# First left operands split straight from PSUM, softmax heads after the stick-breaking heads, and grouped first panels

## The chip, the cores and the metric

The kernel runs on one core of a Trainium2 chip. The metric is the device time of one execution in microseconds (us), as the median of several runs.

## The reference, cut to what matters

A two-layer decoder trunk on one sequence of 2048 tokens and 1024 channels, in float32. Layer 0 ("even") has four softmax heads with a forgetting bias and four stick-breaking heads, 128 wide; layer 1 ("odd") has three groups of eight dilated window heads, 64 wide.

```python
def even_layer(x, g_norm, w_in, b_f, g_q, g_k, w_out):
    proj = rmsnorm(x, g_norm) @ w_in                    # 1024 x 4100
    fq, fk, fv, f_logit, sq, sk, sv, gate = jnp.split(proj, ...)
    fox = forgetting_attention(rmsnorm(fq, g_q), rmsnorm(fk, g_k), fv, log_sigmoid(f_logit + b_f))
    sb = stick_breaking_attention(sq, sk, sv)           # w = beta * prod of (1 - beta) of later keys
    return x + (concat(fox, sb) * silu(gate)) @ w_out   # 1024 x 1024
def odd_layer(x, g_norm, w_in, g_q, g_k, w_out):
    q, k, v, gate = jnp.split(rmsnorm(x, g_norm) @ w_in, ...)   # 1024 x 5120
    att = dilated_window_attention(rmsnorm(q, g_q), rmsnorm(k, g_k), v)
    return x + (att * silu(gate)) @ w_out
```

## The kernel before, in words

**Number form.** Every operand of a large matmul is kept as two parts, hi (a rounded copy, made by ScalarE or GpSimd) and lo (the rest, made by VectorE or GpSimd by a subtraction); `K.split` makes both. A product then is three matmuls (`K.mm3`, L91 to L93: hi·hi, hi·lo, lo·hi).

**Panels.** A projection is done in two rounds of 1024 tokens (`ROUND`), and in each round in panels of 512 output columns. A panel is one 2x2 block multiplication in seven products (Strassen-Winograd): the left operands `A[A11] A[A12] A[S2] A[S3] A[S1] A[A22] A[S4]` are blocks of 512x512 of the activations or sums of them, and each has a weight operand made the same way from the panel's four weight blocks `b11 b12 b21 b22`. `panel` (L240 on) runs the seven products in the order A11, S2, A12, S3, S1, A22, S4 and adds the parts up: `u` and `u3` are kept sums, `result` gives one finished quarter to `emit`, which writes it to DRAM. A product has 24 matmuls 512 wide (mode "d": sq, sk, g0, g1) or 48 matmuls 256 wide (mode "t").

**Weights.** `Weights` loads the four blocks of a panel into four buffers `wraw` (512 KB each), makes sums in place on GpSimd (L210) and splits them into `wop` tiles, two for each product, of which there are four buffers; so weights are at most two products ahead of the matmuls.

**Left operands.** `left_direct` makes the seven left operands of the first round of layer 0 from x: the eight token tiles (`xa`: 0 to 3, `xb`: 4 to 7) are normalised by VectorE, transposed by TensorE (L137), multiplied by the gain when they are copied out of PSUM into `fa` and `fb`, and then split. A11 and A12 need only `xa`; the other five need both. `left` makes the operands of all other rounds from a transposed copy in DRAM (`hT`, or `mixT` for the mixed heads): `stage` holds the first block, `lp` tiles the pieces of the second. In the odd layer's second round it works without a stage.

**The sequence.** `even_projection` (two rounds of the panels sq, sk, sv, fv, fk, fq, g0, g1), then `even_attention` (32 softmax units, kind "f", then 32 stick-breaking units, kind "s"; each unit is 256 queries of one head), then `odd_layer`: two rounds of the output projection (two panels each, `residual` adds x and stores x1), with `transpose_to` normalising and transposing x1 into `hT` for the odd projection, two rounds of the odd projection (ten panels each) with the dilated attention between the products, and the final merge. In a unit `qk` makes the scores and weights (`rows`), and `pv`, two units later, transposes them (L785), splits them (`pT`) and multiplies them with the values into `po`. In the softmax units VectorE adds the bias and takes the running maximum (L740); in the stick-breaking units ScalarE makes two sigmoids (L746, L747) and VectorE a scan (L750).

**Order.** Instructions of one engine run in the order in which they stand. The order comes from a list scheduler of the framework, which follows the program order as priority, with `high_priority` for the evictions of PSUM (`plus`, `copy`). PSUM has four banks "s" (products, scores, `po`) and four banks "t" (transposes and others). DMAs are all issued by one queue (SP), in its order.

Of the kernel before, what the change touches and what calls it, by code (L numbers as in the profile page):

```python
# [17 lines left out]
P = 128  # L18
# [18 lines left out]
class K:  # L37
# [57 lines left out]
    def rstd(self, ss, n, width):  # L95

        nc, sm = self.nc, self.small
# [71 lines left out]

A11, A12, S2, S3, S1, A22, S4 = range(7)  # L170
ORDER = (A11, S2, A12, S3, S1, A22, S4)
FIRST = (A11, A12, S2, S3, S1, A22, S4)
ROUND = S // 2
# [3 lines left out]
class Weights:  # L177


    def __init__(self, k, panels, first=False):  # L180
        self.k, self.ready, self.first = k, [], first
        self.loads = ((w, seg, i, q) for i, (w, seg) in enumerate(panels) for q in ("11", "12", "22", "21"))
        self.raw = {}
        self.loaded = 0
        self.gen = self.prepare(panels)

    def load(self, upto):
        nc = self.k.nc
        while self.loaded < upto:
            self.loaded += 1  # L190
            nxt = next(self.loads, None)
            if nxt is None:
                return
            w, seg, i, q = nxt
            n = sum(c[1] for c in seg[0])
            raw = self.k.raws.tile([P, 4, n], F32, name="wraw", tag="raw")
            rows = slice(0, CH) if q[0] == "1" else slice(CH, D)
            at = 0
            for c0, m in seg[int(q[1]) - 1]:
                nc.sync.dma_start(raw[:, :, at:at + m], w[rows, c0:c0 + m].rearrange("(k p) n -> p k n", p=P))  # L200
                at += m
            self.raw[i, q] = raw

    def prepare(self, panels):
        k, nc = self.k, self.k.nc
        for i, (w, seg) in enumerate(panels):
            n = sum(c[1] for c in seg[0])
            self.load(4 * i + 4)
            b11, b21, b12, b22 = [self.raw.pop((i, q)) for q in ("11", "21", "12", "22")]
# [8 lines left out]
            for j, (src, work) in enumerate(steps[a] for a in (FIRST if self.first and i == 0 else ORDER)):  # L218
                for h in range(2):
                    s = slice(2 * h, 2 * h + 2)  # L220
                    for args in work:
                        tt(*args, s)
                    t = k.wps.tile([P, 2, 2, n], F32R, name="wop", tag="wp")
                    k.split(t[:, :, 0], t[:, :, 1], src[:, s], "act", "pool" if j in (1, 3, 5) else "dve")
                    self.ready.append(t)
                    yield
                if j >= 3:
                    self.load(4 * i + 2 + j)
# [9 lines left out]

def panel(k, A, W, mode, emit, tick, after=None, n=256, first=False):

# [51 lines left out]
    def kept(name):  # L292
        t = k.w4([P, ng, width], name=name, tag=name)
        return [t[:, g] for g in range(ng)]

    u, u3 = kept("u"), kept("u3")
# [99 lines left out]
def left_direct(k, x, A):  # L396

    nc = k.nc
    tt = lambda o, a, b, op: nc.vector.tensor_tensor(o, a, b, op=op)

    def load(xs, b):
        for t in range(TPC):
            for z in range(2):
                c = slice(z * CH, (z + 1) * CH)
                nc.sync.dma_start(xs[:, t, c], x[(b * TPC + t) * P:(b * TPC + t + 1) * P, c])

    def transposed(xt, F, i, on_dve=()):
        k.transposed(xt, k.ge, lambda z: F[:, z * 4:(z + 1) * 4, i], on_dve=on_dve)

    def put(j, i, src, hi_on="pool"):  # L410
        k.split(A[j][:, :, 0, i], A[j][:, :, 1, i], src, hi_on, "dve")

    xa, xb = (k.big([P, TPC, D], name=n) for n in ("xa", "xb"))
    load(xa, 0)
    yield
    load(xb, 1)
    fb, fa = (k.big([P, KT, CH], name=n) for n in ("fb", "fa"))
    A.extend([None] * 7)
    new = lambda *js: [A.__setitem__(j, k.big([P, 4, 2, CH], F32R, name=f"A{j}")) for j in js]
    new(A11, A12, S2)  # L420
    tiles = [xa[:, t] for t in range(TPC)] + [xb[:, t] for t in range(TPC)]
    k.normalise(tiles[0], "dve")
    for t, xt in enumerate(tiles):
        i = slice(t % TPC * P, (t % TPC + 1) * P)
        if t + 1 < len(tiles):
            k.normalise(tiles[t + 1], "dve")
# [5 lines left out]
        transposed(xt, fb, i)  # L432
        s = k.c2([P, 4, P], name="s2")
        tt(s, fb[:, :4, i], fb[:, 4:, i], OP.add)
        tt(s, s, fa[:, :4, i], OP.subtract)
        put(S2, i, s, "act")
    for j, src in ((S3, fa[:, :4]), (S1, fb[:, :4]), (A22, fb[:, 4:]), (S4, fa[:, 4:])):
        new(j)
        for kk in range(4):
            if j == S3:  # L440
                tt(fa[:, kk], fa[:, kk], fb[:, kk], OP.subtract)
            if j == S1:
                nc.gpsimd.tensor_tensor(fb[:, kk], fb[:, kk], fb[:, 4 + kk], op=OP.add)
            if j == A22:
                nc.gpsimd.tensor_tensor(fa[:, 4 + kk], fa[:, 4 + kk], fb[:, 4 + kk], op=OP.subtract)
            if j == S4:
                nc.gpsimd.tensor_tensor(fa[:, 4 + kk], fa[:, 4 + kk], fa[:, kk], op=OP.add)
            k.split(A[j][:, kk, 0], A[j][:, kk, 1], src[:, kk], "act", "dve")


def constants(k, cp, even_norm, odd_norm, even_b_f, even_q_gain, even_k_gain, odd_q_gain, odd_k_gain):
# [4 lines left out]
    k.ident = cs.tile([P, P], F32, name="ident")  # L456
    nc.vector.tensor_scalar(k.ident, jp, 0.0, None, op0=OP.is_equal)
# [87 lines left out]
def even_projection(k, x, w, first, first_left):  # L545
# [14 lines left out]
    def spare():  # L560
        turn[0] += 1
        return ring[0][:, turn[0] % KT]
# [3 lines left out]
    def qk_fox(dst, gain):  # L566
# [5 lines left out]
        def one(block, half, g, src, rs):  # L572
# [8 lines left out]
            k.split(hl[0], hl[1], pt, scale=gain)  # L581
# [39 lines left out]
    def forget():  # L621
# [28 lines left out]
        ("fk", plain(512), "t", qk_fox(k.fT["k"], k.gk)),  # L650
        ("fq", plain(0), "t", qk_fox(k.fT["q"], k.gq)),
# [3 lines left out]
    W = Weights(k, [(w, seg) for _ in range(2) for _, seg, _, _ in kinds], True)  # L655
    W.ahead(1)
    for _ in first:
        pass
    A = first_left
    tick = Pace()  # L660
    tick.every = 2
    for r in range(2):
        B = []
        nxt = left(k, T, 1, B)
        ring[0] = k.big([P, KT, CH], F32R, name="ring")
        for name, seg, mode, emit in kinds:
            if r == 0 and name == "fv":
                tick.add(staggered(k.transpose_to(T, x, t, k.ge) for t in range(TPC * 2, NTT)))
            last = r == 0 and name == "g1"
            panel(k, A, W, mode, emit, tick, (lambda j: next(nxt)) if last else None,  # L670
                  258 if name == "fv" else 256, r == 0 and name == "sq")
# [17 lines left out]
def even_attention(k, tail):  # L689
# [81 lines left out]
    def pv(kind, h, u, rows):  # L771

        vt = heads[kind, h][1]
        po = k.ps("s")
# [31 lines left out]
    k.table()  # L806
# [11 lines left out]
    units = [(kind, h, u) for kind in "fs" for h in range(4) for u in range(NU)]  # L818
    order = [(kind, h) for kind in "fs" for h in range(4)]
# [6 lines left out]
    for n, (kind, h, u) in enumerate(units):  # L826
# [3 lines left out]
        if n + 1 < len(units):  # L830
            q = load_q(*units[n + 1])
        nxt = order.index((kind, h)) + 1
# [12 lines left out]
    tail()  # L845
# [4 lines left out]
def odd_layer(k, x, x1, even_w_out, w_in, w_out, out):  # L850
# [7 lines left out]
    W = Weights(k, outs * 2 + [(w_in, cols(*j)) for js in rounds for j in js])  # L858
    A = []
    yield W, (left(k, k.mixT, 0, A))  # L860
# [13 lines left out]

    for r in range(2):
# [358 lines left out]
```

## Time and profile before

| | |
|---|---|
| median of 3 runs | 2847.14 us (2842.7 to 2855.95) |
| the profiled execution | 2848.43 us, its span 2846.3 us |
| mean granted TensorE clock | 0.98 |
| TensorE busy | 2678.1 us (94%) |
| VectorE busy | 2051.4 us (72%) |
| ScalarE busy | 1649.6 us (58%) |
| GpSimd busy | 1247.2 us (44%) |
| DMA | 437.37 MB, mean 154 GB/s |

Busy times are from the profile's first part. TensorE is PE there, its weight load PEld, VectorE DVE, ScalarE ACT, GpSimd POOL, the DMA queue SPq. A stall of TensorE is seen in three ways: as idle time in a table of stretches, as a row of the waits (who waited for whom, in total, how often, the longest), and as fewer matmuls in a stretch than TensorE does at its full rate.

### The profile page before, as it was taken

The page shows a single profiled execution, that of the slowest core. Times are in us where ns is not written, and L with a number is a line of the kernel's source. Part 1 is how long each engine was busy: PE and PEld are TensorE (multiplying, and loading weights), DVE is VectorE, ACT ScalarE, POOL GpSimd, SP SyncE. Part 2 cuts the span into 40 slices and gives each one's busy share as a digit, 9 for nine tenths or more (in the row PEclk, how much of TensorE's full clock was granted, in tenths as well). Part 3 has the DMA queues.
Part 4 walks back from the last instruction along what each step waited for, and adds up shares of the span by engine and source line. Part 5 has one row for each costly group of instructions (what it writes and reads, how often), then busy time and mean ns, then how long its engine had stood idle before and what let it go on. Part 6 is the DMA issues. An engine that isn't in the chain of part 4 may idle for free.

```text
span 2846.3 us, 55611 instructions
## 1 busy us (share of the span) xinstructions
PE 2678.1 (94%) x20191; PEld 2452.8 (86%) x20191; DVE 2051.4 (72%) x4384; ACT 1649.6 (58%) x3992; POOL 1247.2 (44%) x996
## 2 busy tenths in 40 slices
PE   4999999999999999998887999999989999999998
PEld 3899878998799988887887999999989999999877
DVE  7747885566588788888957857566697586763876
ACT  5446454465466677776364565555665577665642
POOL 5545465444233254456645645353345442422322
PEclk9999999999999999998998999999999999999999
DMA  3557535535644444313667463434533445444675
GB/s 119 167 165 239 189 126 178 163 120 177 189 138 138 138 130 123 112 60 93 200 218 224 144 186 114 131 102 148 173 113 107 142 143 169 127 146 139 214 248 194
DMA packets 388161, 437.37 MB, mean 154 GB/s; under 512 B 31472, under 2 KB 319536, under 8 KB 387888
## 3 DMA queue, kind: packets, MB, share of 16 engines
q1 hardware_dynamic: 387888, 433.83, 48.0%
q8 instruction: 159, 2.61, 0.4%
q14 instruction: 114, 0.93, 0.1%
HBM read 279.16 MB, written 154.57 MB: 152 GB/s over the span
## 4 chain that ended last, share of the span: by engine, by line
PE 46%; DVE 16%; DMA 6%; ACT 4%; issue 3%; POOL 1%; SPq 0%; DVEq 0%; ACTq 0%; POOLq 0%
PE ps L91 12%; PE ps L92 12%; PE ps L93 12%; PE ps L785 3%; DVE rest L750 2%; PE ps L1038 2%; PE ps L1028 2%; DVE wop L86 2%; PE ps L1009 1%; DVE S L86 1%; PE ps L954 1%; DVE A L86 1%; DVE pT L86 1%; DVE lp L319 1%; DMA fin<-uu 1%
## 5 line engine op out<-in xcount | busy, mean ns | idle before, releaser
L210 POOL TENSOR_TENSOR wraw<-wraw 128x512 f32<-128x512 f32 (+1 forms) x320 | 445.3, 1399 | 482.8 <-DVE wop L86 194.2
L81 ACT ACTIVATE wop<-wraw 128x512 fp32r<-128x512 f32 (+1 forms) x560 | 350.6, 630 | 368.0 <-PE ps L93 304.4
L86 POOL TENSOR_TENSOR wop<-wraw,wop 128x512 fp32r<-128x512 f32 (+1 forms) x240 | 329.4, 1375 | 505.6 <-ACT wop L81 484.8
L91 PE MATMUL ps<-wop,S 128*128 128x256 f32 (+1 forms) x1792 | 518.9, 290 | 18.3 <-DVE c L277 9.6
L92 PE MATMUL ps<-wop,S 128*128 128x256 f32 (+1 forms) x1792 | 513.6, 287 | 10.8 <-DVE wop L86 8.1
L92 PE MATMUL ps<-wop,A 128*128 128x256 f32 (+1 forms) x1792 | 512.2, 286 | 8.0 <-DVE wop L86 5.8
L91 PE MATMUL ps<-wop,A 128*128 128x256 f32 (+1 forms) x1792 | 511.3, 286 | 6.4 <-ACT u L282 3.1
L93 PE MATMUL ps<-wop,S 128*128 128x256 f32 (+1 forms) x1792 | 513.9, 287 | 0.0
L93 PE MATMUL ps<-wop,A 128*128 128x256 f32 (+1 forms) x1792 | 509.2, 284 | 0.0
L86 DVE TENSOR_TENSOR wop<-wraw,wop 128x512 fp32r<-128x512 f32 (+1 forms) x320 | 268.9, 841 | 236.1 <-ACT wop L81 233.4
L91 PEld LDWEIGHTS ps<-wop,S 128*128 128x128 f32 x1792 | 343.1, 192 | 24.0 <-DVE c L277 9.9
L92 PEld LDWEIGHTS ps<-wop,S 128*128 128x128 f32 x1792 | 344.5, 192 | 13.7 <-DVE wop L86 9.0
L92 PEld LDWEIGHTS ps<-wop,A 128*128 128x128 f32 x1792 | 342.9, 191 | 10.0 <-DVE wop L86 6.7
L91 PEld LDWEIGHTS ps<-wop,A 128*128 128x128 f32 x1792 | 341.2, 191 | 11.1 <-issue 4.0
L93 PEld LDWEIGHTS ps<-wop,S 128*128 128x128 f32 x1792 | 344.2, 192 | 3.3 <-issue 2.6
L93 PEld LDWEIGHTS ps<-wop,A 128*128 128x128 f32 x1792 | 343.0, 191 | 1.4 <-issue 0.9
L277 DVE TENSOR_TENSOR c<-u,ps 128x512 f32<-128x512 f32 (+1 forms) x254 | 165.1, 657 | 95.6 <-PE ps L93 86.7
L81 ACT ACTIVATE pT<-ps 128x512 fp32r<-128x512 f32 (+2 forms) x352 | 162.4, 504 | 119.0 <-PE ps L785 65.5
L753 POOL TENSOR_TENSOR rows<-rows,rest 128x512 f32<-128x512 f32 (+4 forms) x160 | 153.3, 966 | 153.1 <-DVE rest L750 147.3
L1021 ACT ACTIVATE row<-row,nm 128x256 f32<-128x256 f32 (+1 forms) x384 | 172.4, 451 | 59.1 <-DVE nm L1019 58.6
L86 DVE TENSOR_TENSOR pT<-ps,pT 128x512 fp32r<-128x512 f32 (+2 forms) x352 | 186.5, 559 | 24.6 <-ACT pT L81 23.5
L92 PE MATMUL ps<-pT,vt 128*128 128x256 f32 (+1 forms) x576 | 177.1, 308 | 7.6 <-DVE pT L86 7.3
(216 smaller groups left out, 6557.6 us busy)
## 6 DMA issues: line engine op xcount, KB each, us to landing
wraw<-in_odd_w_in_dram SPq DMA_DIRECT2D x80, 512.0 KB, 4.1
wraw<-in_even_w_in_dram SPq DMA_DIRECT2D x64, 512.0 KB, 4.5
ld<-qk SPq DMA_DIRECT2D x106, 256.0 KB, 3.3
qk<-c SPq DMA_DIRECT2D x96, 256.0 KB, 2.4
lp<-hT SPq DMA_DIRECT2D x60, 256.0 KB, 3.5
uu<-ot SPq DMA_DIRECT2D x96, 132.0 KB, 1.9
fin<-uu SPq DMA_DIRECT2D x16, 792.0 KB, 4.6
hT<-te SPq DMA_DIRECT2D x48, 256.0 KB, 4.2
```

Of the source, the lines that this page charges most:

```text
L81: nc.scalar.activation(hi, src, AF.Copy)
L86: (nc.vector if lo_on == "dve" else nc.gpsimd).tensor_tensor(lo, src, hi.bitcast(F32), op=OP.subtract)
L91: mm(out, a[0], b[0], start=start, stop=False, skip_group_check=more)
L92: mm(out, a[0], b[1], start=False, stop=False, skip_group_check=more)
L93: mm(out, a[1], b[0], start=False, stop=stop, skip_group_check=more)
L210: tt = lambda e, o, x, y, op, s: e.tensor_tensor(o[:, s], x[:, s], y[:, s], op=op)
L277: nc.vector.tensor_tensor(out[g], x[g], y[g], op=OP.add)
L750: nc.vector.tensor_tensor_scan(o[:, b:b + n][:, ::-1], back, k.ident[:, :1].to_broadcast([P, n]), 1.0 if carry is None else carry, OP.mult ...
L753: nc.gpsimd.tensor_tensor(dst[:, :w], dst[:, :w], o[:, b + 1:b + 1 + w], op=OP.mult)
L785: nc.tensor.transpose(pt[:, (jx * 2 + i) * P:(jx * 2 + i + 1) * P], rows[:, i, (jj * 2 + jx) * P:(jj * 2 + jx + 1) * P], k.ident)
L1021: nc.scalar.activation(row[:, h // 2, h % 2, :nk], row[:, h // 2, h % 2, :nk], AF.Exp, bias=nm[:, h:h + 1], accum_out=ot[:, HW + HG + h:HW ...
L1028: nc.tensor.transpose(pp[:, i * P:(i + 1) * P], row[:, h // 2, h % 2, b], k.ident)
```

## The change

1. **First left operands from PSUM.** The gain is loaded as a row to all partitions (`gb`) and multiplied into the tile together with the root on VectorE, so that the transposed tile in PSUM is final: the hi part (ScalarE) and the lo part (VectorE) are made from PSUM. The squares of two tiles share one chain for their roots. x comes in whole tiles, the weights follow right behind `xa`, and the small constants come after the first panels' first products (`late`, `identity`).
2. **Groups.** `Weights` takes group sizes. In a group, the products A11 and A12 of all its panels come first, and the five others of each panel follow; the blocks b11 and b21 are loaded a second time for them (22 more loads of 512 KB). Groups are the first three panels of layer 0, the two panels of each output round, and the first two panels of each odd round. In a group's panel A12 goes to banks of its own and is added to `u` by VectorE, where before the products were summed in PSUM and copied out by ScalarE.
3. **Left operands beside the group.** The second half of `left_direct` and the later pieces of the first `left` of the odd layer are stepped by `Pace` between these first products. `tail`, which makes the first operands of the output projection, is called in units 5 and 6 of the last head instead of after the last unit.
4. **Heads.** The stick-breaking heads come first, the softmax heads last; `po` of the stick-breaking units takes a "t" bank. The activation tables are loaded by hand at other places (9 loads stand in the program, 23 before).

```diff
-    k.normalise(tiles[0], "dve")
-    for t, xt in enumerate(tiles):
...
-            transposed(xt, fa, i, (1,))
-            put(A11, i, fa[:, :4, i])
-            put(A12, i, fa[:, 4:, i])
+    squares(0)
+    ahead = {0: (1,), 1: (2, 3), 3: (4, 5), 5: (6, 7)}
+    for t in range(2 * TPC):
+        scaled(t)
+        if t in ahead:
+            squares(*ahead[t])
+        p0, p1 = transposed(t)
         if t < TPC:
+            for z, j in enumerate((A11, A12)):
+                put(j, i, (p0, p1)[z])
+                nc.scalar.activation(fa[:, z * 4:(z + 1) * 4, i], (p0, p1)[z], AF.Copy)
+            if t == TPC - 1:
+                yield
             continue
+        nc.scalar.activation(s1, p0, AF.Copy)
+        tt(a, a, p0, sub)
+        tt(s, p1, a, sub)
+        put(S2, i, s)
+        put(A22, i, p1)
+        tt(s1, p1, s1, plus)
+        tt(fa[:, 4:, i], fa[:, 4:, i], s, sub, nc.gpsimd)
+        yield
...
 class Weights:
+            if n == 1:
+                self.parts.append((these[0], ORDER))
+            else:
+                self.parts += [(i, EARLY) for i in these] + [(i, FIRST[2:]) for i in these]
...
     if first:
         result(0, 0, u, product(A12, fresh()))
+        yield
+        u3 = kept("u3")
         plus(u, u, product(S2, fresh()))
...
-    W = Weights(k, [(w, seg) for _ in range(2) for _, seg, _, _ in kinds], True)
+    W = Weights(k, [(w, seg) for _ in range(2) for _, seg, _, _ in kinds], [3] + [1] * 13)
+    opened = [panel_steps(k, A, W, mode, emit, pace, first=tag) for (_, _, mode, emit), tag in zip(kinds, tags)]
+    for p in opened:
+        next(p)
+    late()
+    pace.finish()
...
-        po = k.ps("s")
+        po = k.ps("s" if kind == "f" else "t")
...
-    units = [(kind, h, u) for kind in "fs" for h in range(4) for u in range(NU)]
+    units = [(kind, h, u) for kind in "sf" for h in range(4) for u in range(NU)]
...
-    tail()
+        if nxt == len(order) and u in (5, 6):
+            tail()
...
-        for n in range(2):
-            panel(k, A, W, "t", residual(r, n), tick, (lambda j: next(nxt)) if n == 1 else None)
-            if r == 1 and n == 0:
-                tick.finish()
+        both = two(A, [residual(r, n) for n in range(2)], pace if r == 0 else tick,
+                   lambda j: None if j in EARLY else next(nxt))
+        next(both)
+        if r == 0:
+            pace.finish()
+            next(nxt)
+            next(nxt)
+        next(both)
+        if r == 1:
+            tick.finish()
+            next(nxt)
+            next(nxt)
+        next(both)
```

TensorE at the program's start, before: `ident,xa` and `ident,xb` are the transposes of the token tiles (eight for a tile), `A_169` is A11 of the first panel.

```order
L137 MATMUL ps<-ident,xa 128x128 x32
L137 MATMUL ps<-ident,xb 128x128 x16
L91 MATMUL ps<-A_169,wop 128x512 x2
L92 MATMUL ps<-A_169,wop 128x512
L93 MATMUL ps<-A_169,wop 128x512
```

The same of the changed kernel, around the end of its first product: `A_127` is A11, `A_128` is A12.

```order
L92 MATMUL ps<-A_127,wop 128x512
L93 MATMUL ps<-A_127,wop 128x512
L469 MATMUL ps<-ident,xb 128x128 x8
L91 MATMUL ps<-A_128,wop 128x512
L92 MATMUL ps<-A_128,wop 128x512
```

The transposes of the second four tiles stood ahead of the first product or behind the second; now eight stand behind each of the first four products (A11, A12, A11, A12), two more products of A11 and A12 follow, and S2 is the seventh product (it was the third).

ScalarE of the changed kernel, up to the last hi part that the first product needs (`A_127`, `A_128`: hi parts; `junk`: squares; `fa`: a copy for the later operands; `lg`, `r`: chain of the roots):

```order
L106 ACTIVATE lg<-ms 128x2
L81 ACTIVATE wop<-wraw 128x2x256 x2
L487 ACTIVATE fa<-ps 128x4x128
L108 ACTIVATE r<-lg 128x2
L81 ACTIVATE A_127<-ps 128x4x128
L81 ACTIVATE A_128<-ps 128x4x128
L487 ACTIVATE fa<-ps 128x4x128 x2
L455 ACTIVATE junk,ssx<-xb 128x1024 x2
L81 ACTIVATE A_127<-ps 128x4x128
L106 ACTIVATE lg<-ms 128x2
L81 ACTIVATE A_128<-ps 128x4x128
L108 ACTIVATE r<-lg 128x2
```

The fourth `A_127` is the next row. Ahead of it stand, from the start, 6 squares, 8 of the roots' chain, 6 hi parts, 4 copies `fa` and 4 weights `wop`; before, GpSimd made the hi parts of A11 and A12.

ScalarE at the end of the second output round, before: `te` copies the last transposed tiles of x1 to be stored as `hT`, `A_17343` and `A_17410` are A11 and A12 of the first odd round, `S_17475` its S2, `c` a result of the panel that is running.

```order
L144 ACTIVATE te<-ps,go 128x128 x16
L282 ACTIVATE c<-ps 128x512
L81 ACTIVATE wop<-wraw 128x2x256 x2
L282 ACTIVATE c<-ps 128x512
L81 ACTIVATE A_17343<-stage 128x512 x4
L81 ACTIVATE wop<-wraw 128x2x256 x2
L81 ACTIVATE A_17410<-stage 128x512 x4
L81 ACTIVATE S_17475<-lp 128x512 x3
```

And of the changed kernel (`A_17358`, `A_17367`, `S_17433` are the same operands):

```order
L133 ACTIVATE xt<-xt,r_17030 128x1024
L81 ACTIVATE wop<-wraw 128x2x256
L149 ACTIVATE te<-ps,go 128x128 x8
L81 ACTIVATE wop<-wraw 128x2x256 x5
L81 ACTIVATE A_17358<-stage 128x512 x4
L81 ACTIVATE wop<-wraw 128x2x256
L81 ACTIVATE A_17367<-stage 128x512 x4
L81 ACTIVATE S_17433<-lp 128x512 x3
```

Between the last `te` and the first part of A11 stood two weights (one product), and now stand five (two and a half products); and S2 is needed as the fifth product of the odd round, where it was the second.

More of the change, by code (lines that the diff above doesn't have):

```diff
@@ L172 @@
 FIRST = (A11, A12, S2, S3, S1, A22, S4)
+EARLY = FIRST[:2]
 ROUND = S // 2
@@ L183, in __init__, with load @@
         self.raw = {}
-        self.loaded = 0
-        self.gen = self.prepare(panels)
-    def load(self, upto):
+        self.gen = self.prepare()
+    def load(self):
         nc = self.k.nc
[L189 to L202, printed above, removed]
@@ L204, in prepare @@
-    def prepare(self, panels):
-        k, nc = self.k, self.k.nc
[L206 to L209, printed above, removed]
+        nxt = next(self.loads, None)
+        if nxt is None:
+            return
+        at, i, q = nxt
+        w, seg = self.panels[i]
+        n = sum(c[1] for c in seg[0])
+        raw = self.raw[at, q] = self.k.raws.tile([P, 4, n], F32, name="wraw", tag="raw")
@@ new lines, in load, with prepare @@
+        rows = slice(0, CH) if q[0] == "1" else slice(CH, D)
+        at = 0
+        for c0, m in seg[int(q[1]) - 1]:
+            nc.sync.dma_start(raw[:, :, at:at + m], w[rows, c0:c0 + m].rearrange("(k p) n -> p k n", p=P))
+            at += m
+    def prepare(self):
+        k, nc = self.k, self.k.nc
+        for _ in range(4):
+            self.load()
+        for at, (i, js) in enumerate(self.parts):
+            n = sum(c[1] for c in self.panels[i][1][0])
+            b11, b21, b12, b22 = [self.raw.pop((at, q), None) for q in ("11", "21", "12", "22")]
@@ L217, in prepare @@
             }
-            for j, (src, work) in enumerate(steps[a] for a in (FIRST if self.first and i == 0 else ORDER)):
+            for a, j in enumerate(js):
+                src, work = steps[j]
                 for h in range(2):
@@ L236, in get, with panel, panel_steps @@
         return self.ready.pop(0)
-def panel(k, A, W, mode, emit, tick, after=None, n=256, first=False):
+def panel(*args, **kw):
+    for _ in panel_steps(*args, **kw):
+        pass
+def panel_steps(k, A, W, mode, emit, tick, after=None, n=256, first=None):
     nc = k.nc
@@ L423, in left_direct, with squares, scaled @@
-    for t, xt in enumerate(tiles):
+    new(A11, A12, S2, A22)
+    roots = {}
+    def squares(*ts):
+        ss = k.small.tile([P, 8], F32, name="ssx", tag="ss4")
+        for j, t in enumerate(ts):
+            nc.scalar.activation(k.c2([P, D], BF, name="junk"), tiles[t], AF.Square, accum_out=ss[:, j:j + 1])
+        r = k.rstd(ss, 8, D, len(ts))
+        for j, t in enumerate(ts):
+            roots[t] = r[:, j:j + 1]
+    def scaled(t):
+        nc.vector.scalar_tensor_tensor(tiles[t], tiles[t], roots[t], gb, op0=OP.mult, op1=OP.mult)
@@ L542, in staggered, with even_projection @@
         yield
-def even_projection(k, x, w, first, first_left):
+def even_projection(k, x, w, first, first_left, early, late):
     tc, nc = k.tc, k.nc
@@ L654, in even_projection @@
     ]
-    W = Weights(k, [(w, seg) for _ in range(2) for _, seg, _, _ in kinds], True)
+    W = Weights(k, [(w, seg) for _ in range(2) for _, seg, _, _ in kinds], [3] + [1] * 13)
     W.ahead(1)
-    for _ in first:
-        pass
+    next(first)
     A = first_left
+    ring[0] = early
+    pace = Pace()
+    pace.every = 2
+    pace.add(first)
+    tags = ("u", "x", "x")
+    opened = [panel_steps(k, A, W, mode, emit, pace, first=tag) for (_, _, mode, emit), tag in zip(kinds, tags)]
[3 more added lines that the diff above has]
+    pace.finish()
     tick = Pace()
@@ L817, in even_attention @@
     NU = NTT // 2
[L818 to L819 removed]
+    units = [(kind, h, u) for kind in "sf" for h in range(4) for u in range(NU)]
+    order = [(kind, h) for kind in "sf" for h in range(4)]
     chunk = load_head(*order[0])
@@ L873, in residual, with two @@
         return each(emit)
+    def two(A, emits, tick, after=None):
+        ps = [panel_steps(k, A, W, "t", emit, tick, after if n else None, first=("u", "x")[n])
+              for n, emit in enumerate(emits)]
+        for p in ps:
+            next(p)
+        yield
+        for p in ps:
+            next(p, None)
+            yield
     for r in range(2):
```

150 lines of the change are left out of this document (90 added, 60 removed).

## The prediction

> **What bounds the kernel now.** I read the busy shares first, then a table of eight stretches, then TensorE's waits, then the timeline where most is lost.
>
> ```profile
> PE 2678.1 (94%) x20191; PEld 2452.8 (86%) x20191; DVE 2051.4 (72%) x4384; ACT 1649.6 (58%) x3992; POOL 1247.2 (44%) x996
> core 0: us, PE busy (x) PEld busy (x) DVE busy (x) ACT busy (x) POOL busy (x), PEclk, DMA share, GB/s
> 0.00:100.00 100.00, 57.68 (x236) 45.55 (x237) 82.31 (x155) 54.55 (x135) 52.95 (x44) 0.93 0.37 117
> 100.00:746.00 646.00, 624.57 (x4073) 565.33 (x4071) 407.47 (x648) 330.67 (x623) 314.35 (x245) 0.99 0.54 172
> 746.00:1003.00 257.00, 255.58 (x1841) 232.35 (x1842) 206.19 (x673) 160.87 (x356) 82.18 (x96) 0.99 0.49 150
> 1003.00:1300.00 297.00, 276.72 (x1915) 239.52 (x1912) 260.10 (x364) 218.97 (x496) 149.98 (x158) 0.99 0.34 106
> 1300.00:1600.00 300.00, 250.27 (x1878) 244.06 (x1879) 245.26 (x322) 149.08 (x314) 171.12 (x110) 0.90 0.57 181
> 2050.00:2150.00 100.00, 89.50 (x763) 82.84 (x763) 91.04 (x181) 64.06 (x161) 45.84 (x31) 0.95 0.38 119
> 100.00:140.00 40.00, 40.00 (x182) 32.73 (x181) 24.80 (x32) 17.84 (x30) 23.24 (x18) 1.00 0.60 204
> 140.00:200.00 60.00, 60.00 (x506) 60.00 (x505) 28.36 (x45) 24.20 (x45) 28.58 (x22) 1.00 0.50 145
> ```
>
> TensorE bounds most stages, and no matmul is removed, so only its idle time can go. It sits at four places: the start (42 us idle of 100), the stick-breaking heads (1003 to 1300: 20 idle, VectorE 88% busy), their end with the output projections (1300 to 1600: 50 idle and the granted clock at 0.90) and the odd round boundary (10 idle). The softmax heads (746 to 1003) lose 1.4. The last two rows are the full rates: 182 matmuls 512 wide in 40 us (0.22 us each, a product of 24 in 5.3 us), 506 of 256 in 60 us (a product of 48 in 5.7 us). By the second, the 1878 matmuls of 1300 to 1600 need 223 us, so 77 are lost there.
>
> ```profile
> PE ps L1028 <- DVE ot L1015: 15.1, 5, 7.4
> PE ps L92 <- DVE wop L86: 13.9, 6, 5.1
> PE ps L91 <- DVE rest L750: 13.8, 24, 2.0
> PE ps L91 <- DVE c L277: 11.3, 5, 6.1
> PE ps L137 <- issue: 11.2, 1, 11.2
> PE ps L137 <- DVE xa L130: 10.9, 2, 9.9
> PE ps L91 <- ACT A L81: 8.7, 2, 8.3
> PE ps L92 <- DVE A L86: 3.7, 1, 3.7
> PE ps L785 <- DVE pT L86: 1.1, 6, 0.2
> ```
>
> Nearly all of it is waiting for VectorE or ScalarE, which make operands.
>
> **The change part by part.** *Start.* The first product stands late, because operands are late:
>
> ```profile
> 4.61 1.06 ACT L126 ACTIVATE junk<-xa 128x1024 bf16<-128x1024 f32 x1 [2.60 <-DMA xa<-in_x_dram]
> 7.02 1.06 ACT L126 ACTIVATE junk<-xa 128x1024 bf16<-128x1024 f32 x1 [0.84 <-DMA xa<-in_x_dram]
> L126 ACT ACTIVATION_READ_ACCUMULATOR junk<-xa 128x1 f32 x4 | 0.7, 186 | 0.0
> 14.45 8.32 SPq L405 DMA_DIRECT2D xb<-in_x_dram  x8
> 40.24 1.20 PE L91 MATMUL ps<-A,wop 128*128 128x512 f32 x2
> L86 DVE TENSOR_TENSOR A<-fa,A 128x512 fp32r<-128x512 f32 x16 | 17.3, 1103 | 0.0
> L277 DVE TENSOR_TENSOR c<-u,ps 128x512 f32<-128x512 f32 (+1 forms) x254 | 165.1, 657 | 95.6 <-PE ps L93 86.7 <-DMA gg<-c 3.7 <-DMA qk<-c 3.1
> L81 ACT ACTIVATE A<-fa 128x512 fp32r<-128x512 f32 x8 | 4.7, 621 | 3.0 <-DVE fa L399 3.0
> L101 ACT ACTIVATE lg<-ms 128x1 f32<-128x1 f32 x10 | 2.0, 202 | 12.6 <-DVE ms L99 12.4
> L91 PE MATMUL ps<-A,wop 128*128 128x512 f32 x58 | 24.6, 438 | 9.7 <-ACT A L81 8.7 <-DVE r L109 1.0
> ```
>
> Now ScalarE's queue decides. Ahead of the last hi part of A11 stand 6 squares (1.06 and some 0.2 for reading the sum), 8 steps of the roots (0.20), and 15 passes over 512 columns (6 hi, 4 `fa`, 4 `wop`, the last hi: 0.62): 7.5 + 1.6 + 9.3 = 18.4 us. From the first tile's landing at 4.6, with 2 us for the gain row that lands ahead of tile 1 (a tile's 512 KB came every 2.4 us), the first product starts near 25, not 40.2. GpSimd, which made those hi parts, is free. VectorE's lo parts now come from PSUM (0.66 as `c`, where `A<-fa` took 1.10 beside a busy GpSimd).
>
> Before, the first 100 us held 172 product matmuls (58 and two like it; x236 less 64 transposes). After: 100 − 25 − 6 (32 transposes of `xb`) − 8 of stalls (between 2 and the 12 that followed the first product before: 8.7 and 3.7) = 61 us, 278 matmuls. 106 more at 0.22 us: −23 us. Six early products (33 us) cover the operands of the second half: some 40 VectorE passes, 26 us at 0.66 and 44 at 1.10. If these are all slow and the first product comes at 32, 11 are left; at 21 with stalls of 2, 33.
>
> The trace has no VectorE pass with two tensors over 1024 columns (`scaled`); I take twice 0.66, against 0.75 for the pass without the gain row:
>
> ```profile
> 9.06 0.75 DVE L130 TENSOR_SCALAR xa<-xa,r 128x1024 f32<-128x1024 f32 x1
> L142 DVE TENSOR_SCALAR fa<-ps,ge 128x128 f32<-128x128 f32 x16 | 4.5, 338 | 0.0
> ```
>
> Eight times 0.57 is 4.6 more, against 4.5 (L142) saved: nothing. The Trainium skill speaks against reading PSUM here: "VectorE: DVE Perf Modes", section "Rules for kernel authors", says to accept the slow single-rate mode on a matmul's output or copy it to SBUF first when many operations follow, and here three or four do. Taken as a price, double the time of the 24 VectorE passes from PSUM, it would add 16 us to VectorE in the start and leave about −9 there. The trace does not bear that out for passes with two tensors: 657 ns from PSUM, 1103 from SBUF.
>
> *Output projections and the step into the odd layer.* Two products stood ahead of S2's need, now four do, in three places, so S2, S3 and the rest have 23 us of cover instead of 6:
>
> ```profile
> 1505.88 1.14 ACT L144 ACTIVATE te<-ps,go 128x128 f32<-128x128 f32 x4 [1.50 <-DMA hT<-te]
> 1520.13 2.19 ACT L81 ACTIVATE A<-stage 128x512 fp32r<-128x512 f32 x4 [3.62 <-DMA stage<-hT]
> 1515.00 0.80 PE L91 MATMUL ps<-wop,S 128*128 128x256 f32 x2 [6.36 <-ACT wop L81]
> 1541.00 0.58 PE L91 MATMUL ps<-wop,S 128*128 128x256 f32 x1 [6.12 <-DVE c L277]
> L86 DVE TENSOR_TENSOR A<-stage,A 128x512 fp32r<-128x512 f32 x32 | 38.2, 1238 | 2.5 <-ACT A L81 2.5
> L871 DVE TENSOR_TENSOR x1t<-c,x1t 128x512 f32<-128x512 f32 x32 | 33.6, 1058 | 13.5 <-DMA x1t<-in_x_dram 13.2 <-DVE c L277 0.3
> ```
>
> ScalarE stood at `stage` for a DMA with weights queued behind it, and TensorE waited 6.4 us for those; five weights now stand between `te` and `stage`, two before. What is late next is VectorE: its 245 busy us stay, less some 16 passes (A11, A12, parts of S2 and S3) that move into the softmax heads' end, where it is 80% busy: 245 − 16·1.1 = 227. It was idle for 55 us there, partly for the chain x1, `xt`, `te`, `hT`, `stage`, which stays serial; I keep 40 of them. 300 − 267: −33 us. At best TensorE's 223 is reached (−77; VectorE's 227 excludes it, so −70); at worst VectorE's order moves the same stalls (−5).
>
> *Odd round boundary*: the same with a group of two, 10.5 us idle, VectorE 91 of 100 busy: −6 (0 to −10).
>
> *Heads.* TensorE's waits for the scan (13.8) are waits for an "s" bank, of which `po` took one. VectorE at 260 of 297 leaves at most 37 to gain. On the other side the first units start with no `pv` beside them and the transposes get three banks. The mix may come out at −12 or +12: −2.
>
> *Costs.* 20 results go from ScalarE's copies to VectorE (0.66 each, 13 us); off the path except at VectorE's crowded places: +3 (0 to 13). 22 more loads of 512 KB: hidden behind a DMA share of about half; uncovered they would cost their landing:
>
> ```profile
> wraw<-in_odd_w_in_dram SPq DMA_DIRECT2D x80, 512.0 KB, 4.1
> L210 POOL TENSOR_TENSOR wraw<-wraw 128x512 f32<-128x512 f32 (+1 forms) x320 | 445.3, 1399 | 482.8 <-DVE wop L86 194.2
> L103 ACT ACT_TABLE_LOAD x8 | 10.3, 1283 | 0.1
> ```
>
> 14 fewer table loads of 1.28 us, off the path but for a few in the second round: −2 (0 to −5).
>
> Sum: −23 − 33 − 6 − 2 + 3 − 2 = −63. From the profiled execution's 2848.4 (span and 2.1 around it), 1.3 above the median of the runs: 2785, as a median 2784.
>
> **Rivals.** *Slower:* transposes of the stick-breaking heads wait for a "t" bank that `po` holds. 4 heads x 36 steps = 144 bank requests. At 0.43 us each the change is worth nothing (61/144); at 0.53 it ends at 2860. For it: VectorE is the crowded engine there and must clear those banks. Against: all such waits were 1.1 us with four banks.
>
> *VectorE is the bound of the output projections,* and regrouping gives only −5 there and nothing at the odd boundary: 2848 − 29 = 2819. For it: 245 busy of 300. Against: it was idle 55 us, while TensorE waited.
>
> *The start comes late:* ScalarE's two squares of `xb` stand ahead of two hi parts; if `xb` lands as late as before or VectorE runs at 1.10 throughout, −11 there: 2796. Against: no constants are queued ahead of the weights and `xb` any more.
>
> *The group's own weights are late:* S2's need a second load and four GpSimd sums behind it, 4.1 + 4·1.4 = 9.7 us at five groups, 48 in all: 2832. That is, the change doesn't do what it says. Against: loads follow each early product, two products ahead.
>
> *PSUM reads at half rate* (the mechanism of the page): −9 in place of −23: 2798.
>
> **How the numbers follow.** Forecast 0.60 (own range 2752 to 2812), start late 0.14, VectorE bound 0.13, weights late 0.05, PSUM 0.03, slower 0.05. A measurement of this kernel tells about 0.5% (14 us) from no change. Faster by more: the first three and PSUM, 0.90; the weights' case lies at the border (same 0.05); slower 0.05. The 8 in 10 take in the forecast and most of the first two rivals: 2750 to 2825.
>
> **What would show it.** First product's matmul at about 25 us and about 280 product matmuls in the first 100 us; TensorE idle under 30 us between the last head and the odd layer's first five products; the wait of the odd boundary (`ot`) halved; the transposes' waits for a bank in the stick-breaking heads still near 1 us. The prediction fails if VectorE is found 95% busy through the output projections, or if the stick-breaking stage (297 us) grows by over 15.

## The result and the profile after

The changed kernel takes 2826.16 us (median of 6 runs, 2821.26 to 2831.74) against 2851.36 beside it: ratio 0.9917, 95% interval 0.9901 to 0.9933. By the ratio that is 24 us, where 63 were forecast (2784); the time lies 1 us outside the range, which ended at 2825. First the busy shares, then stretches of the changed kernel and, below them, those of before that answer to the 1300s to 1600s and to the odd boundary.

```profile
PE 2676.4 (95%) x20191; PEld 2455.5 (87%) x20191; DVE 2052.7 (73%) x4373; ACT 1618.6 (57%) x3924; POOL 1223.4 (43%) x981
core 0: us, PE busy (x) PEld busy (x) DVE busy (x) ACT busy (x) POOL busy (x), PEclk, DMA share, GB/s
0.00:100.00 100.00, 76.36 (x376) 63.58 (x377) 79.30 (x130) 57.23 (x113) 40.99 (x36) 0.95 0.54 172
713.00:1007.00 294.00, 267.71 (x1789) 232.67 (x1787) 247.95 (x343) 216.13 (x482) 148.85 (x157) 0.98 0.39 117
1300.00:1400.00 100.00, 83.58 (x676) 82.07 (x676) 90.65 (x101) 42.23 (x76) 68.30 (x43) 0.95 0.59 189
1400.00:1500.00 100.00, 91.00 (x716) 89.40 (x715) 63.55 (x113) 60.57 (x149) 40.24 (x31) 0.93 0.76 250
1500.00:1600.00 100.00, 78.24 (x601) 77.25 (x601) 90.12 (x125) 47.07 (x104) 65.89 (x42) 0.88 0.59 190
2016.00:2200.00 184.00, 172.34 (x1465) 163.45 (x1464) 150.60 (x289) 102.62 (x251) 80.61 (x57) 0.95 0.43 137
```

```profile
1320.00:1420.00 100.00, 86.91 (x662) 84.63 (x661) 91.33 (x97) 43.41 (x78) 63.52 (x39) 0.93 0.54 167
1420.00:1520.00 100.00, 83.31 (x644) 81.20 (x643) 56.88 (x102) 59.46 (x147) 44.09 (x30) 0.93 0.67 210
1520.00:1620.00 100.00, 85.84 (x676) 84.94 (x675) 97.14 (x130) 47.74 (x98) 69.40 (x45) 0.91 0.55 179
2040.00:2224.00 184.00, 169.76 (x1466) 160.84 (x1465) 145.10 (x285) 104.29 (x256) 81.28 (x57) 0.97 0.40 125
```

The start gained: TensorE is busy for 76 us of the first 100, where it was for 58. The output projections and the odd boundary look as before: VectorE is full at both ends (about 91 and 90 to 97 of 100), has air only in the middle (57 and 64), and TensorE loses as much.

To say where the time went I cut each profiled execution at the same products: the 280 products were counted by their matmuls with `wop` (a product is 24 of 512 or 48 of 256 columns). Each stretch runs from the start of one product to the start of another. The table gives the us from the program's start to the tenth product; from there to the last product of the first projection; to the first output product; 43 products on, into the first odd panels; and the 23 products around the odd boundary. e1 and so on are the experiments below.

| kernel | to 10th | projection | heads | output, step | odd boundary |
|---|---|---|---|---|---|
| before | 110.3 | 624.3 | 585.6 | 329.1 | 183.6 |
| changed | 89.0 | 618.1 | 590.3 | 327.9 | 183.7 |
| e1 no late groups | 89.8 | 618.8 | 590.1 | 327.4 | 184.5 |
| e2 GpSimd relieved | 89.9 | 619.1 | 585.8 | 318.2 | 184.0 |
| e2b sums left out | 89.9 | 618.7 | 593.4 | 303.9 | 182.4 |
| e3 lo parts left out | 89.7 | 618.5 | 582.6 | 302.9 | 184.8 |
| e4 weights first | 88.5 | 618.1 | 588.8 | 326.5 | 185.2 |
| e5 = e1 + e2 | 89.1 | 620.5 | 591.5 | 311.0 | 185.9 |
| e6 softmax first | 88.9 | 620.1 | 583.6 | 337.4 | 183.5 |
| e7 relieved wide | 89.9 | 618.6 | 590.1 | 318.5 | 169.4 |
| e8 start alone | 90.1 | 624.5 | 583.3 | 325.6 | 185.4 |
| e9 before, relieved | 108.8 | 623.8 | 583.1 | 310.9 | 174.8 |
| e10 = e5 + odd boundary | 89.6 | 616.7 | 588.4 | 313.9 | 174.6 |
| e11 relieved everywhere | 89.2 | 610.9 | 587.9 | 315.2 | 170.0 |
| e12 = e11, no late groups, old heads | 89.1 | 610.5 | 580.1 | 317.2 | 173.3 |
| e13 = e11, no late groups | 89.6 | 610.4 | 586.1 | 309.6 | 177.9 |

Changed against before: −21.3, −6.2, +4.7, −1.2, +0.1; the rest holds a few us. One execution of a stretch varies by some us (the heads above all), so only differences that several kernels repeat are used.

TensorE's waits in the changed kernel between 1283 and 1640 us (who waits for whom, total, times, longest), and then the work of VectorE and of GpSimd ahead of the 8.4 us:

```profile
PE ps L92 <- DVE wop L86: 18.3, 7, 8.4
PE ps L91 <- DVE c L300: 16.6, 3, 10.3
PE ps L142 <- ACT xt L133: 6.8, 3, 2.9
```

```profile
1327.50 6.77 DVE L86 TENSOR_TENSOR S<-stage,S 128x512 fp32r<-128x512 f32 x4
1334.19 1.75 DVE L86 TENSOR_TENSOR S<-lp,S 128x512 fp32r<-128x512 f32 x1
1335.87 1.75 DVE L86 TENSOR_TENSOR A<-lp,A 128x512 fp32r<-128x512 f32 x1
1337.54 0.68 DVE L86 TENSOR_TENSOR wop<-wraw,wop 128x512 fp32r<-128x512 f32 x1
...
1328.66 1.72 POOL L345 TENSOR_TENSOR lp<-lp 128x512 f32<-128x512 f32 x1
1330.34 5.05 POOL L226 TENSOR_TENSOR wraw<-wraw 128x512 f32<-128x512 f32 x3
1335.36 1.71 POOL L86 TENSOR_TENSOR wop<-wraw,wop 128x512 fp32r<-128x512 f32 x1
1338.36 1.60 POOL L226 TENSOR_TENSOR wraw<-wraw 128x512 f32<-128x512 f32 x1 [1.29 <-DVE wop L86]
```

TensorE waited 8.4 us, until 1338, for the `wop` at 1337.54. The reading that matters: four VectorE passes took 6.77 us, 1.69 each, in step with GpSimd's passes of 1.7. The moment GpSimd paused (at 1337.1), a VectorE pass of the same size took 0.68. So a pair of one pass each takes 1.7 us when the engines run together; VectorE alone would do both in some 1.36 (an estimate: twice 0.68). The Trainium skill, "SBUF — State Buffer", section "Who interferes with whom", has the rule: a VectorE pass with two inputs in SBUF and a GpSimd pass that reads SBUF exclude each other by a lock, and the second waits until the first is done. The trace agrees in kind: VectorE's pass grows from 0.68 to 1.69 beside GpSimd. In size it shows less: GpSimd's sums took 1.29 where no VectorE pass ran beside them (median of 34 in the whole trace), so two passes strictly one behind the other would take 1.97, and the pair took 1.7.

The longest wait, 10.3 us until 1517.8, was for the `c` that stands last here:

```profile
1506.78 3.43 DVE L86 TENSOR_TENSOR A<-stage,A 128x512 fp32r<-128x512 f32 x2
1510.14 1.74 DVE L86 TENSOR_TENSOR S<-lp,S 128x512 fp32r<-128x512 f32 x1
1511.80 1.75 DVE L954 TENSOR_TENSOR x1t<-c,x1t 128x512 f32<-128x512 f32 x1
1513.47 2.35 DVE L86 TENSOR_TENSOR S<-lp,S 128x512 fp32r<-128x512 f32 x2
...
1516.95 0.67 DVE L300 TENSOR_TENSOR c<-u,ps 128x512 f32<-128x512 f32 x1
```

VectorE did not stand still in that time. Five of its passes took some 1.75 us while GpSimd worked until 1514.7; at 0.68 they would have been done 5 us sooner.

### The profile page after: what moved, and what is told of

It reads as the page before. It is cut to its first block, busy times and chain, and to the rows that moved or that the text cites. A ratio compares the mean times of both kernels' runs of the same rounds, so it can differ in the third digit from the quotient of the medians.

```text
span 2824.8 us, 55621 instructions
## 1 busy us (share of the span) xinstructions
PE 2676.4 (95%) x20191; PEld 2455.5 (87%) x20191; DVE 2052.7 (73%) x4373; ACT 1618.6 (57%) x3924; POOL 1223.4 (43%) x981
## 4 chain that ended last, share of the span: by engine, by line
PE 62%; DVE 21%; DMA 7%; ACT 5%; issue 3%; POOL 1%; SPq 1%; DVEq 0%; ACTq 0%; POOLq 0%
PE ps L91 17%; PE ps L93 17%; PE ps L92 17%; DVE rest L828 4%; PE ps L863 2%; PE ps L1145 2%; DVE wop L86 2%; DVE A L86 2%; PE ps L1135 2%; PE ps L1116 2%; DVE lp L345 1%; DVE S L86 1%; PE ps L1061 1%; DVE pT L86 1%; DVE c L300 1%
## 5 line engine op out<-in xcount | busy, mean ns | idle before, releaser
L91 PEld LDWEIGHTS ps<-wop,S 128*128 128x128 f32 x1792 | 342.1, 191 | 15.1 <-issue 8.4
L300 DVE TENSOR_TENSOR c<-u,ps 128x512 f32<-128x512 f32 (+1 forms) x274 | 178.7, 659 | 91.9 <-PE ps L93 86.1
L92 PE MATMUL ps<-pT,vt 128*128 128x256 f32 x576 | 171.1, 299 | 5.5 <-DVE pT L86 5.3
```

The lines of the kernel that those rows point to most:

```text
L91: mm(out, a[0], b[0], start=start, stop=False, skip_group_check=more)
L92: mm(out, a[0], b[1], start=False, stop=False, skip_group_check=more)
L300: nc.vector.tensor_tensor(out[g], x[g], y[g], op=OP.add)
```

## The experiments

Ratios are to the kernel before, run beside each.

**e1: late groups undone.** Output and odd panels run one by one; start, heads and tables stay changed.

```diff
-                [2, 2] + [2, 1, 1, 1, 1, 1, 1, 1, 1] * 2)
+                [1] * 4 + [1] * 20)
-        both = two(A, [residual(r, n) for n in range(2)], ...
+        for n in range(2):
+            panel(k, A, W, "t", residual(r, n), tick, ...)
```

> The groups of the output rounds and of the odd rounds are undone: their panels run one after the other as before the change, their weights are loaded once, and the left operands stand ahead of the first product. The start with its group of three, the heads' order and the place of A11 and A12 in the last head stay. Theory of the prediction (four early products cover S2 and S3, and what they won in the output rounds was lost somewhere else): about 2826 + 33 + 6 - 3 = 2862 us, and the 43 products from the first output product to the odd layer's sixteenth take 33 us more than with the groups (328 us). Theory W (VectorE has the same work to do either way and is full in bursts; the groups only move the stalls): 2826 within 8 us, and those 43 products take 328 within 8.

2830.63 us, 0.9921 (0.9907 to 0.9936): the same as with groups, and 327.4 in the output stretch. The term of −33 is nothing. VectorE was busy there for 259 us, with the groups for 268: the groups took no work off it.

**e2: GpSimd relieved in the output rounds.**

```diff
-            tt = lambda e, o, x, y, op, s: e.tensor_tensor(...)
+            free = i < self.free            # the four output panels
+            tt = lambda e, o, x, y, op, s: (nc.vector if free else e).tensor_tensor(...)
-                    ... "pool" if a in (1, 3, 5) else "dve")
+                    ... "pool" if a in (1, 3, 5) and not free else "dve")
```

and in `left` the operations with `nc.gpsimd` go to VectorE likewise.

> In the four output panels and in the three sets of left operands made meanwhile, GpSimd's work (weight sums, lo parts of three products in a panel, sums of left operands: 86 passes) is given to VectorE. Between 1283 and 1593 us VectorE's 354 passes lasted 273 us together; at the median of the passes of the same form with no GpSimd pass beside them they would last 198. Theory W (the number of VectorE's passes sets the pace): 86 more at 0.68 us are 58 us more work for the full engine, so slower, 2826 + 30 to 50. Theory L (VectorE is slow because GpSimd runs beside it, a pass of 0.68 us then taking 1.0 to 1.75): 198 + 58 = 256 us of VectorE, less than the 273 now, so the time is the same or up to 15 us better, 2811 to 2830, and the mean of the lo passes of weights falls to about 0.7 us in the stage.

**e2b: GpSimd's sums left out there** (`for args in () if i < self.bare else work`, and likewise in `left`; the clamp of the odd layer's gate is −40 in place of −80, which changes no work).

> GpSimd's sums for the weights of the four output panels and for the three sets of left operands made meanwhile are left out (the operands are split from what lies there; 62 passes fewer); the gate's clamp is -40 in place of -80. VectorE does the same passes as in the changed kernel. Theory L (GpSimd beside VectorE makes the stalls): VectorE's passes shorten by some 50 us in the stage and most of the stalls go: 2826 - 25 to - 45. Theory W in its strict form (the number of VectorE's passes): no change, 2826 within 5. Theory Q (order in VectorE's queue: left operands stand ahead of weights): a small gain, 5 to 10 us, since the weights' sums no longer delay the lo parts.

**e3: lo parts of the left operands left out there**, in the output rounds and the first odd round; the third matmul of each trio repeats the second, so TensorE does as many.

```diff
-        k.split(t[:, kk, 0], t[:, kk, 1], src, "act", "dve")
+        nc.scalar.activation(t[:, kk, 0], src, AF.Copy)
```

> The lo parts of the left operands of the two output rounds and of the first odd round are left out (84 VectorE passes of 128x512 fewer); the third matmul of each trio there repeats the second, so TensorE does the same number. Theories W and L: VectorE is the bound, 84 passes of 0.7 to 1.25 us are 60 to 105 us off it, and nearly all of the stage's stalls go: 2826 - 35 to - 60. If the stalls are made by ScalarE, the DMA chain (x1, xt, te, hT, stage) or the weights' loads, the gain is under 15 us.

e2: 2818.48, 0.9877 (0.9862 to 0.9893). e2b: 2802.53, 0.9824 (0.9808 to 0.9840). e3: 2800.75, 0.9807 (0.9784 to 0.9830). The output stretch falls from 328 to 318, 304 and 303. VectorE's largest groups of passes between 1283 and 1592 us, in the changed kernel and then in e2:

```profile
L86 DVE TENSOR_TENSOR wop<-wraw,wop 128x512 fp32r<-128x512 f32 x44 | 40.6, 927 | 11.0 <-ACT wop L81 10.9
L954 DVE TENSOR_TENSOR x1t<-c,x1t 128x512 f32<-128x512 f32 x32 | 31.8, 998 | 9.0 <-DMA x1t<-in_x_dram 8.9
L300 DVE TENSOR_TENSOR c<-u,ps 128x512 f32<-128x512 f32 x41 | 27.5, 678 | 3.0 <-ACT u L305 1.9 <-PE ps L93 0.9
```

```profile
L86 DVE TENSOR_TENSOR wop<-wraw,wop 128x512 fp32r<-128x512 f32 x69 | 51.7, 758 | 9.5 <-ACT wop L81 9.4
L957 DVE TENSOR_TENSOR x1t<-c,x1t 128x512 f32<-128x512 f32 x32 | 21.7, 682 | 5.6 <-issue 2.8 <-DMA x1t<-in_x_dram 2.6
L228 DVE TENSOR_TENSOR wraw<-wraw 128x512 f32<-128x512 f32 x32 | 20.9, 683 | 7.3 <-DMA wraw<-in_even_w_out_dram 7.2
```

`x1t` fell from 998 to 682 ns; `c` (one input in PSUM) had been 678 all along, and in the whole trace of the changed kernel it took 680 even where GpSimd was busy beside it (median of 99). More work for the fullest engine made the kernel faster, so the count of VectorE's passes (theory W in its strict form) does not set the pace; that they grow long beside GpSimd (theory L) is the reading that fits. How much of e2's 10 us is due to it stays open: VectorE's busy time in the stretch only fell from 268 us to 263, and a weight's sum, which takes GpSimd 1.47 us there, takes VectorE 0.68, so that the chain to the weights is shorter as well. e2b takes away both too. The longest wait above, at least, was VectorE's own queue. e3 shows that VectorE's work counts: without the lo parts 25 us come back in the output stretch.

**e4: weights ahead of left operands** (`high_priority(URGENT)` around the weights' `split` from the output rounds on).

> All parts of the weights of the output rounds and of the odd layer get the same raised priority as the evictions, so that they stand ahead of left operands in VectorE's, ScalarE's and GpSimd's queues wherever both could come next. Theory Q (VectorE's order made the stalls: in the changed kernel TensorE waited 8.4 us in one piece for a lo part of weights that stood behind three parts of left operands): the waits for wop, 18.3 us between 1283 and 1600, go below 6 and nothing takes their place: 2826 - 12 to - 20. Theory L (VectorE's time is used up by its passes and by standing still beside GpSimd): the waits for wop turn into waits for results and left operands, 2826 within 6.

2833.02, 0.9926 (0.9910 to 0.9942): no gain. Waits in e4, in the same stretch as those of the changed kernel above:

```profile
PE ps L92 <- DVE wop L86: 27.0, 7, 9.2
PE ps L142 <- ACT xt L133: 10.1, 4, 4.3
PE ps L91 <- DVE c L301: 2.4, 3, 1.6
```

The wait for results fell from 16.6 to 2.4, those for weights and `xt` grew from 25 to 37. This order in the queues moves the stalls and does not shrink them: theory Q, as tried here, falls.

**e5: e1 and e2 together.**

> Output and odd panels without groups (2830.6 us in that experiment), and GpSimd's work of the output panels and of the left operands on VectorE, as in the kernel with groups (2818.5, against 2826 with the work on GpSimd). If GpSimd beside VectorE costs the same in both orders (theory L): 2830.6 - 8 = 2822, within 4. If it was GpSimd that kept the groups from paying (the prediction's step is right once VectorE is not held up): no gain here, 2829 to 2840, and the groups are worth over 10 us with VectorE free.

2813.89, 0.9859 (0.9843 to 0.9876). Relief pays at least as much without groups, so it was not GpSimd that kept the groups from paying here; in the output stretch (311 without them, 318 with them) they pay in neither case.

**e6: the old order of heads in the changed kernel** (`"fs"` for `"sf"`).

> The heads stand in the order of before (softmax first, stick-breaking last); all else is as in the changed kernel, po of the stick-breaking units in a bank t. The stretch from the last product of the first projection to the first output product took 585.6 us before and 590.3 after. Theory 1 (the order of heads costs those 5 us, the softmax heads at the end lengthen by 19 and the stick-breaking ones gain 9 and the drain 4): about 2821. Theory 2 (the last head now also makes the first left operands, and in stick-breaking units, where VectorE was 88% busy, that costs more than in softmax units): 2830 to 2845.

2832.21, 0.9927 (0.9907 to 0.9947), not told apart from the changed kernel. The heads gained 7 us and the output stretch lost 9.5, in one execution. That the first output operands now fell among stick-breaking units, where VectorE is fuller, would explain the loss; it was not tested by itself.

**e7: relief also at the start and around the odd boundary** (`left` without a stage, odd panels 1, 2, 10, 11, 12).

> As the kernel that gives GpSimd's work of the output panels to VectorE (2818.5 us), and the same for the first three panels of the start, for the left operands of the second odd round and for the odd panels around its boundary and the first two odd ones. Theory L: at the odd boundary VectorE was busy 92 of 100 us with GpSimd busy 45; passes at 0.68 in place of 1.0 to 1.75 give 5 to 10 us there and 2 to 5 in the start: 2804 to 2814. Theory W (VectorE's passes count): some 60 passes more in full stretches, 2818 + 10 to + 30.

2804.91, 0.9837 (0.9822 to 0.9853). Nothing at the start; at the boundary 183.7 became 169.4:

```profile
2008.00:2178.00 170.00, 167.45 (x1461) 158.89 (x1460) 144.89 (x318) 102.19 (x245) 34.40 (x25) 1.00 0.46 147
```

VectorE makes 318 passes where it made 289, in less busy time (144.9, not 150.6), and TensorE idles 3 us in place of 12.

**e8: the new start alone on the kernel before; e9: relief alone on the kernel before** (output rounds and odd boundary).

> The kernel before with the new start alone (left operands from PSUM, group of three panels, constants later); heads, their po, the place of the first output operands, the table loads, the output and the odd panels as before. If the start carries the change (the first product stood 16.5 us earlier, the tenth 21.3, and the distance stayed at 21 to 33 us to the end): 2851 - 21 = 2830, within 4, that is all but a few us of the whole change. If what the start wins is given back where VectorE is full: 2840 or more.

> The kernel before with one thing changed: in the four output panels, in the odd panels 1, 2, 10, 11 and 12 and in the left operands made around them GpSimd's sums and lo parts are given to VectorE. Theory L (a GpSimd pass holds VectorE up for longer than VectorE would take for it): 10 to 17 us in the output rounds, as in the two kernels with and without groups, and some 13 at the odd boundary: 2851 - 23 to - 30, that is 2821 to 2828, as much as the whole change gives. Theory W (VectorE's passes count): 2851 + 20 or more.

e8: 2828.33, 0.9918 (0.9904 to 0.9933), the whole change's ratio. e9: 2821.96, 0.9899 (0.9883 to 0.9916): to give VectorE what GpSimd did, with no regrouping at all, is worth as much as the whole change.

**e10: e5 with the relief of the odd boundary; e11: relief in every panel, on the changed kernel.**

> The changed kernel without the groups of the output and odd rounds (start, heads and tables as changed), and with GpSimd's work at the output rounds and at the odd boundary given to VectorE. Without groups and with that work moved in the output rounds alone it was 2813.9; the odd boundary gave 13.7 us in the kernel with groups (products 208 to 231 took 226.5 us in place of 240.2). If the groups are worth nothing in the odd layer either: 2800, within 5. If the groups pay there once VectorE is free: 2808 to 2815.

> The changed kernel with all of GpSimd's work for weights and left operands given to VectorE, in every panel: some 320 sums of 0.68 us, 217 us, and the lo parts besides, on an engine that was busy for 2052 of 2825 us. Theory L: 2795 to 2806 (as the kernel that moved it at the crowded places alone, 2804.9, with a few us more at the remaining boundary). Theory W: the odd layer's panels, with VectorE busy 55 to 75% and evictions behind the sums, lengthen: 2815 to 2850.

e10: 2809.21, 0.9854 (0.9837 to 0.9870): 9 us above the value for groups that are worth nothing, and inside the 2808 to 2815 set for groups that pay at the odd boundary once VectorE is free. The table bears that out: with relief the boundary takes 169 and 170 us with groups (e7, e11) and 173 to 178 without (e9, e10, e12, e13). The output stretch goes the other way, 315 to 319 with groups and 310 to 317 without, so that in total little is left. e11: 2800.62, 0.9820 (0.9800 to 0.9840), 26 us better than the changed kernel. VectorE went from 2052.7 to 2144.7 us busy, GpSimd from 1223.4 to 377.4:

```profile
PE 2666.6 (95%) x20191; PEld 2445.9 (87%) x20191; DVE 2144.7 (77%) x4981; ACT 1625.2 (58%) x3924; POOL 377.4 (13%) x373
```

608 more passes cost VectorE 92 us, 0.15 each, since its other passes grew shorter.

**e12, e13: e11 without late groups, with old and new heads.**

> The new start, the new table load in the first projection, all of GpSimd's work for weights and left operands on VectorE, no groups in the output and odd rounds, and the heads as before the change (softmax first, po in a bank s, first output operands after the last unit). If the new heads cost what the stretches of the kernels with the old and the new heads show (from the last product of the first projection to the forty-fourth after it 909 us with the old ones, 917.5 and 918.2 with the new): 9 us less than its twin with the new heads, about 2790. If that difference is chance of the profiled executions: the same as the twin, within 4.

> The twin of the kernel above with the heads as changed (stick-breaking first, po in a bank t, first output operands in units 5 and 6 of the last head). It is the all-free kernel (2800.6 us) without the groups of the output and odd rounds; groups worth nothing: 2800, within 6.

2798.92, 0.9816 (0.9796 to 0.9836), and 2803.18, 0.9826 (0.9804 to 0.9847): 4 us apart, less than the intervals tell. The new heads took longer in most of the table's rows (586 against 580 here), but the time does not show the +4.7 to be a cost. e13 is not told apart from e11 either: in total, no worth of the late groups can be told even with full relief.

## Why the prediction was right and wrong, step by step

- *Start, −23: right*, −21.3, and in part by luck. These rows of the first 100 us show it (waits, the way to the first product, VectorE's passes to 70 us):

```profile
PE ps L469 <- DVE xa L461: 16.2, 3, 8.1
18.83 2.47 DVE L461 SCALAR_TENSOR_TENSOR xa<-xa,r,gb 128x1024 f32<-128x1024 f32 x2
20.15 3.67 PE L469 MATMUL ps<-ident,xa 128*128 128x128 f32 x16 [4.92 <-DVE xa L461]
23.66 1.10 PE L91 MATMUL ps<-A,wop 128*128 128x512 f32 x2
L86 DVE TENSOR_TENSOR A<-ps,A 128x512 fp32r<-128x512 f32 x12 | 8.2, 686 | 0.4 <-ACT A L81 0.3
L86 DVE TENSOR_TENSOR A<-fa,A 128x512 fp32r<-128x512 f32 x4 | 6.3, 1627 | 0.0
L86 DVE TENSOR_TENSOR wop<-wraw,wop 128x512 fp32r<-128x512 f32 x6 | 4.0, 685 | 0.4 <-ACT wop L81 0.4
```

  The first product stood at 23.7 (forecast 25), but not by the path of the sum. "Now ScalarE's queue decides" held until some 16 us; then the roots' chain and the scaling of two tiles on VectorE and their transposes decided, and ScalarE waited for these transposes with its last hi parts. So the nearness of 25 is partly chance. The other sizes held: TensorE's stalls behind the first product were 7.5 us (taken as 8), `scaled` took 1.28 (taken as 1.32). Of the first 100 us' 312 product matmuls 96 are 256 wide, which the forecast of 280 left out; they count as 264 wide ones. Lo parts from PSUM took 686 ns, as long as those of weights from SBUF (685), and those from SBUF beside GpSimd 1627, so the rival of half rate from PSUM falls. e8, with the start alone, has the whole change's time.
- *Output projections and step into the odd layer, −33: this is the step that failed.* It measured −1.2, and e1 puts it at nothing. The sum was "idle for 55 us there … I keep 40 of them". The 55 us of VectorE's idle time were real, but they lie between two full stretches (91, 57, 97 of 100 before; 91, 64, 90 after), and more products ahead of S2 do not make the full ones emptier: the same passes have to be done there beside the same GpSimd. An average over 300 us hid it. The sum also took VectorE's work there down by 18 us; it was 269 us before and 268 after (e1, without groups: 259), in part because results moved from ScalarE to VectorE in just this stretch (`c`: 41 passes of VectorE, before 30). And S2 had one product ahead of it before, not two, as the 6 us of cover beside it say. The sign named for a failure, VectorE 95% busy, could not warn: it was 82% busy on average and full at both ends. The row with 1.24 us for `A<-stage` stood in the prediction and was used as a price, not as a thing that could be changed.
- *Odd boundary, −6: wrong*, +0.1. The wait for `ot` (10 of its 15.1 us lay here) went, and the time didn't: other waits of the same attention took its place (12 of 184 us idle, before 14), as these rows of 2016 to 2200 us show. e7 shows the cure: with GpSimd relieved the boundary loses 14 us, and e9, without groups, loses 9.

```profile
PE ps L1135 <- ACT uT L1149: 3.4, 1, 3.4
PE ps L1135 <- ACT pT L1137: 3.2, 1, 3.2
```

- *Table loads, −2: too small*, −6.2 in the projection; e8 and e9, which load as before the change, keep 624.
- *Heads, −2, and results on VectorE, +3:* not told from the runs' spread. The scan's waits in the stick-breaking units stayed (before, then after, each in its own stage).

```profile
PE ps L91 <- DVE rest L750: 11.8, 23, 0.9
PE ps L91 <- DVE rest L828: 15.2, 36, 1.8
```

- *Rivals.* "VectorE is the bound" was nearest: it gave −5 and nothing at the boundary. It lacked the reason: many of VectorE's passes are long because of GpSimd. "Slower" by the transposes' bank did not come: no wait of a transpose for a cleared bank is among the rows of that stage, which took 294 us, not 297. Late weights: GpSimd's sums did wait for loads between 1283 and 1600 us, 15.5 in all, but e1, which loads once, has the same stretch.

```profile
POOL wraw L226 <- DMA wraw<-in_even_w_out_dram: 9.8, 6, 3.9
POOL wraw L226 <- DMA wraw<-in_odd_w_in_dram: 5.7, 3, 4.4
```


Open: with the lo parts or the sums left out, the output stretch still takes 303 us, where 43 products at 5.7 would take 245; what is left there was not taken apart.

## What to carry to other kernels

Idle time of an engine counts only where it stands: cut a stage into pieces before promising any of it. When the bound is VectorE and its two-input passes last longer in one stage than elsewhere, look at what GpSimd does at that moment; work given back to VectorE (0.68 us a pass) can be cheaper than work beside it (1.7 a pair). A new order of the same work moves waits; ask for each what is taken off the engine that is waited for.

## What the runs showed of the hardware

Small VectorE passes grow most beside GpSimd. The roots' pass of 128x16 (`r`, L114) took 0.17 us in the 36 cases of the changed kernel with no GpSimd pass beside it and 1.14 in the ten that one covered (medians); a pass of 128x512 goes from 0.68 to some 1.75. And here TensorE paid for a long wait twice. After the longest one:

```profile
1517.77 0.55 PE L91 MATMUL ps<-wop,A 128*128 128x256 f32 x1 [10.34 <-DVE c L300]
1518.12 0.41 PE L92 MATMUL ps<-wop,A 128*128 128x256 f32 x1
...
1523.00 0.28 PE L91 MATMUL ps<-wop,A 128*128 128x256 f32 x1
1523.12 0.28 PE L92 MATMUL ps<-wop,A 128*128 128x256 f32 x1
```

the matmuls start 0.21 us apart for 5 us and then 0.12, while the granted clock of 1500 to 1600 us was 0.88: some 2 us more, on top of the wait of 10.3. After the three next longest waits of that stage (8.4, 5.1 and 4.5 us) the same spacing lasted 3.6 to 5.5 us.
